# Rewritten stage boundaries of a three-block network kernel on one core

## The chip, the cores and the metric

The kernel runs on one core of a Trainium2 chip. The metric is device time in microseconds: how long one execution of the whole program takes on that core. Five engines work in it, each with an instruction stream of its own: TensorE (PE in the profile, with its weight loads as PEld), VectorE (DVE), ScalarE (ACT), GpSimd (POOL) and SyncE (SP), which here issues the DMAs.

## The reference, cut to what matters

Three networks are chained on one sequence of 512 positions and 1024 channels. Each begins or ends its stages with a norm over the channels, and nearly all the arithmetic is dense products of 1024-channel activations with weights.

```python
def rmsnorm(x, g):                       # the second block's differs in the eps alone
    return x * lax.rsqrt(jnp.mean(x * x, axis=-1, keepdims=True) + EPS) * g

def _layernorm(x, g, b):                 # third block
    mu, var = x.mean(-1), ((x - mu) ** 2).mean(-1)
    return (x - mu) * rsqrt(var + 1e-5) * g + b

def reference(x, ...):
    x = first_block(x, ...)    # rmsnorm, z = h @ w_in, convolution and sparse attention, FFN, gate
    x = second_block(x, ...)   # hyena mixer + FFN, rwkv mixer + FFN, final rmsnorm
    return third_block(x, ...)

def third_block(x, ...):
    u = x @ w_in + b_in                                   # split into the inputs of both mixers
    h_a = _head_layernorm(_mlstm_chunkwise(...)) * sigmoid(mo)
    h_b = _head_rmsnorm(_hgrn2_chunkwise(silu(hq), 1 - f, hi, log f)) * sigmoid(hg)   # 8 heads
    mixed = sigmoid(ga) * (h_a @ w_proj_a) + sigmoid(gb) * (h_b @ w_proj_b)
    x = _layernorm(ALPHA * x + mixed @ w_out, ln1_g, ln1_b)
    ffn = (silu(x @ w_ffn_gate) * (x @ w_ffn_up)) @ w_ffn_down
    return _layernorm(ALPHA * x + ffn, ln2_g, ln2_b)
```

## The kernel before

**Layout.** The activation `x` lies transposed in eight tiles of 128 channels by 512 positions. A product in float32 is made of three faster ones: every operand is split into a high half (`wh`, `h`, a rounded copy made by ACT) and a low half (`wl`, `l`, the rest, a subtraction on DVE), and `mm3` adds the products (`wh`,`h`), (`wh`,`l`) and (`wl`,`h`). The trace writes a product as its two inputs, so these read `h,wh`, `l,wh` and `h,wl`. A weight comes in chunks: `wsplit` (lines 151 to 157) loads 128 by 2048 numbers, 1 MB, into a raw tile `wraw`, of which there are three, and makes `wh` and `wl` of it, of which there are two each. `dense_steps` then runs over the eight input tiles `k` and the two column groups of a chunk, three matmuls each: 48 matmuls in a chunk. All loads stand in one queue on SP.

**What sets the order.** The Tile framework's scheduler places the instructions of each engine by its own estimate of time. Where the code says `manual_schedule` for an engine, that engine runs in the order of the code. Tiles lie in pools: a tile of a new pool that falls on the place of an old one waits until the old one's last reader is done. `phase` (lines 109 to 114) opens the weight pool, then the activation pool, then PSUM; it is opened once for the first block and the first half of the second, once in `block2b` for the last FFN of the second block, and once for the third block.

**The start.** `begin` (264 to 273) loads x0 and x1, then the first weight chunk `w1a`, then x2 to x7. `norm_split` splits every x into `h` and `l` (lines 190, 191), squares it on ACT (`sq`, line 218) and sums the squares on POOL (`sqa`, line 223); a matmul with a matrix of ones (`sqa,ones`) sums over the channels, and `rstd_of` makes the reciprocal root of it with one Newton step (194 to 203). The products don't wait for `rstd`, which is multiplied in later.

**Norms at the end of a stage.** `sumsq_soon` (236 to 244) is the same sum with the last tile's square sent to PE by itself, so that only it is late. ACT holds one table of functions, and another function's table costs an `ACT_TABLE_LOAD`; the reciprocal root needs one.

**HGRN2 heads.** `hgrn` runs eight heads in pairs. `head` is a generator that yields between its steps: scores of the diagonal, seven levels of a tree in which DVE masks a level into `hpt` and multiplies `hq` and `hk` by the decay, then the product with the values `po`, a copy `ho`, and the norm of the head: square on ACT, ones matmul, `rstd_of`, two products on DVE. `weave` (line 2127) mixes the steps of two heads with the matmuls of a fill (the input products of the next pair, 24 or 40 steps) by the counts it is given; PE alone runs there in the order of the code.

**Layer norms of the third block.** `LayerNorm` centres the tiles on the mean of the first six (`mean`, `center`), sums their squares on POOL (`lna`), and treats x6 and x7, which are late, apart (`late`): `p1` gathers the sum of the two, `p2` the squares. `finish` (1770 to 1782) takes the rest of the mean off all eight tiles (`dm`; the trace calls that tile `z`), five of them on DVE and three on POOL, makes the variance `w` (in the trace `ct`), then `rstd`, and then multiplies every tile by gain and `rstd` on DVE and adds the bias on ACT. After the first of them (LN1) the FFN splits the eight tiles (`split`, lines 187 and 188); after the second (LN2) they are stored.

## Time and profile before

| what | value |
|---|---|
| median of 3 runs | 4061.11 us (4058.75 to 4064.93) |
| the profiled execution | 4056.95 us, its span 4055.2 us |
| TensorE clock over the span | 0.967 of full |
| busy: PE / DVE / ACT / POOL | 94 / 59 / 40 / 18% |
| chain that ended last | PE 58%, DVE 8%, ACT 3% |

The span is the time from the first to the last instruction of the profiled execution. A row of the timeline gives the start of an instruction, its duration, engine and line, what it writes and reads, and in brackets how long the engine was idle before it and what ended that; rows marked x5 are five alike in a run, with the time from the first's start to the last's end. A window row gives busy time and number of instructions for each engine in a stretch, then the granted clock (1.00 is 2.4 GHz, 0.50 is 1.2 GHz) and the DMA share.

### The profile page before, as it was taken

The page shows a single profiled execution, that of the slowest core. Times are in us where ns is not written, and L with a number is a line of the kernel's source. Part 1 is how long each engine was busy: PE and PEld are TensorE (multiplying, and loading weights), DVE is VectorE, ACT ScalarE, POOL GpSimd, SP SyncE. Part 2 cuts the span into 40 slices and gives each one's busy share as a digit, 9 for nine tenths or more (in the row PEclk, how much of TensorE's full clock was granted, in tenths as well). Part 3 has the DMA queues.
Part 4 walks back from the last instruction along what each step waited for, and adds up shares of the span by engine and source line. Part 5 has one row for each costly group of instructions (what it writes and reads, how often), then busy time and mean ns, then how long its engine had stood idle before and what let it go on. Part 6 is the DMA issues. An engine that isn't in the chain of part 4 may idle for free.

```text
span 4055.2 us, 51969 instructions
## 1 busy us (share of the span) xinstructions
PE 3813.6 (94%) x20982; PEld 2972.9 (73%) x20982; DVE 2390.9 (59%) x3492; ACT 1610.3 (40%) x2182; POOL 726.5 (18%) x574
## 2 busy tenths in 40 slices
PE   8899999999899998889878899999999999998998
PEld 6556888777788883666656688877777888876886
DVE  5965655667866556476665665565554554454334
ACT  3455433455443333343442333355544333323222
POOL 1000200032620016444442100101111000030001
PEclk9899999999999999999988899999999999999999
DMA  6122222222232324544433223132223222332221
GB/s 214 48 78 98 100 86 106 90 94 94 99 110 88 106 82 156 150 112 112 117 92 103 99 78 115 57 136 93 86 93 117 86 79 78 130 127 73 99 87 64
DMA packets 184132, 408.69 MB, mean 101 GB/s; under 512 B 80361, under 2 KB 98314, under 8 KB 155988
## 3 DMA queue, kind: packets, MB, share of 16 engines
q1 hardware_dynamic: 183892, 405.38, 30.0%
q8 instruction: 165, 2.70, 0.3%
q14 instruction: 75, 0.61, 0.0%
HBM read 364.37 MB, written 43.57 MB: 101 GB/s over the span
## 4 chain that ended last, share of the span: by engine, by line
PE 58%; DVE 8%; ACT 3%; DMA 1%; issue 1%; POOL 0%; SPq 0%; DVEq 0%; ACTq 0%; POOLq 0%
PE pacc L138 49%; PE pf L138 3%; PE pb L138 2%; PE ch L138 1%; PE pa L138 1%; DVE ct L1928 1%; DVE wl L157 1%; DVE GB L1418 1%; DVE tw L1470 1%; PE py L138 1%; DVE W L1472 0%; ACT wh L156 0%; PE pb L1440 0%; DVE bk L1378 0%; DVE x L1776 0%
## 5 line engine op out<-in xcount | busy, mean ns | idle before, releaser
L138 PE MATMUL pacc<-h,wh 128*128 128x512 f32 x3792 | 1499.2, 397 | 34.1 <-ACT wh L156 19.9
L138 PE MATMUL pacc<-h,wl 128*128 128x512 f32 x3792 | 1484.7, 393 | 4.1 <-DVE wl L157 4.1
L138 PE MATMUL pacc<-l,wh 128*128 128x512 f32 x3792 | 1486.3, 392 | 1.3 <-DVE l L188 1.2
L138 PEld LDWEIGHTS pacc<-h,wh 128*128 128x128 f32 x3792 | 718.0, 189 | 215.1 <-issue 31.1
L138 PEld LDWEIGHTS pacc<-h,wl 128*128 128x128 f32 x3792 | 716.5, 189 | 163.4 <-DVE wl L157 8.4
L138 PEld LDWEIGHTS pacc<-l,wh 128*128 128x128 f32 x3792 | 717.9, 189 | 151.5 <-issue 3.4
L157 DVE TENSOR_TENSOR wl<-wraw,wh 128x2048 fp32r<-128x2048 f32 (+2 forms) x276 | 610.4, 2212 | 370.1 <-ACT wh L156 370.0
L156 ACT ACTIVATE wh<-wraw 128x2048 fp32r<-128x2048 f32 (+2 forms) x276 | 492.6, 1785 | 789.6 <-PE pacc L138 692.1
L138 PE MATMUL pf<-x,wf 128*128 128x256 f32 x736 | 222.2, 424 | 5.7 <-DMA x<-yd 3.4
L223 POOL TENSOR_TENSOR sqa<-sq 128x512 f32<-128x512 f32 x12 | 19.3, 1609 | 1007.7 <-ACT sq L218 667.8
L138 PEld LDWEIGHTS pf<-x,wf 128*128 128x128 f32 x736 | 131.2, 198 | 41.5 <-issue 11.4
L295 DVE TENSOR_TENSOR z<-pacc,rstd 128x512 f32<-128x512 f32 x132 | 90.2, 691 | 101.3 <-PE pacc L138 101.0
L323 DVE TENSOR_TENSOR x<-pacc,x 128x512 f32<-128x512 f32 x48 | 33.2, 691 | 178.4 <-PE pacc L138 178.4
L223 POOL TENSOR_TENSOR sqa<-sqa,sq 128x512 f32<-128x512 f32 x50 | 100.4, 2008 | 110.1 <-ACT sq L218 102.1
L309 ACT ACTIVATE ct<-ct 128x512 f32<-128x512 f32 x66 | 41.8, 633 | 180.8 <-DVE ct L306 120.4
L138 PE MATMUL pacc<-wh,h 128*128 128x512 f32 (+2 forms) x288 | 103.6, 362 | 9.6 <-DVE z L983 9.6
L1835 POOL TENSOR_TENSOR x<-x,z 128x512 f32<-128x512 f32 x16 | 22.8, 1447 | 456.4 <-DVE z L1834 456.4
L138 PE MATMUL pacc<-wl,h 128*128 128x512 f32 (+2 forms) x288 | 103.2, 358 | 0.4 <-DVE wl L157 0.4
L138 PE MATMUL pacc<-wh,l 128*128 128x512 f32 (+2 forms) x288 | 103.1, 361 | 0.0
L290 DVE TENSOR_TENSOR hv<-ct,pacc 128x512 f32<-128x512 f32 x22 | 15.1, 688 | 143.3 <-PE pacc L138 143.3
L552 DVE SCALAR_TENSOR_TENSOR x<-sg,vecs,x 128x491 f32<-128x491 f32 (+28 forms) x120 | 86.2, 744 | 5.1 <-ACT x L543 4.7
L1421 POOL TENSOR_TENSOR AX<-AX,rwc 64x512 f32<-64x512 f32 x64 | 82.3, 1286 | 33.3 <-ACT AX L1420 29.7
(521 smaller groups left out, 4997.2 us busy)
## 6 DMA issues: line engine op xcount, KB each, us to landing
wraw<-in_w_up_dram SPq DMA_DIRECT2D x44, 1024.0 KB, 4.8
wraw<-in_w_down_dram SPq DMA_DIRECT2D x32, 704.0 KB, 4.0
wraw<-in_w_up2a_dram SPq DMA_DIRECT2D x22, 1024.0 KB, 4.8
wraw<-in_w_up2b_dram SPq DMA_DIRECT2D x22, 1024.0 KB, 4.9
x<-xmd SPq DMA_DIRECT2D x72, 256.0 KB, 2.8
wraw<-in_w1a_dram SPq DMA_DIRECT2D x16, 1024.0 KB, 4.8
wraw<-in_w3q_dram SPq DMA_DIRECT2D x16, 1024.0 KB, 4.8
wraw<-in_hy_w_in_dram SPq DMA_DIRECT2D x12, 1024.0 KB, 4.7
```

Of the source, the lines that this page charges most:

```text
L138: s.nc.tensor.matmul(out, a, b, start=start, stop=stop)
L156: s.nc.scalar.activation(wh[:, :n], raw[:, :n], AF.Copy)
L157: s.nc.vector.tensor_tensor(wl[:, :n], raw[:, :n], wh[:, :n].bitcast(F), op=SUB)
L223: nc.gpsimd.tensor_tensor(a2, acc, q, op=ADD)
L295: nc.vector.tensor_tensor(z, ps, rstd, op=MUL)
L309: nc.scalar.activation(t, t, act)
L323: nc.vector.tensor_tensor(x[n], ps, x[n], op=ADD)
L552: nc.vector.scalar_tensor_tensor(y[:, d:], u[:, :T - d], w, y[:, d:], op0=MUL, op1=ADD)
L1418: nc.vector.tensor_tensor(GB[h, hs], q[h], mask[h, None].to_broadcast([64, 4, 2, 64]), op=MUL)
L1421: nc.gpsimd.tensor_tensor(AX[o, hs, X], AX[o, hs, X], mask[o, None].to_broadcast([64, 4, 2, 64]), op=MUL)
L1470: nc.vector.tensor_tensor(tw[:, 0:i, 0:i], W[:, 0:i, 0:i].rearrange("p j c -> p c j"), L[:, 0:i, i][:, None, :].to_broadcast([P, i, i]), o ...
L1928: nc.vector.scalar_tensor_tensor(t[:, d:], z[:, :T - d], w[3 - d], t[:, d:], op0=MUL, op1=ADD)
```

## The change

It has five parts, and all keep the arithmetic of the outputs up to the order of additions.

1. `begin` loads the first weight in four pieces of 256 KB, one after each even x tile, and splits each piece by itself. A small activation on `ones` stands first on ACT and brings the table load before the data.
2. `phase` can open the activation pool before the weight pool (`weights_last`), and does in two of the three phases. In `block3` the first weight of mLSTM, `w3q`, is loaded and split ahead of the splits of x.
3. `ready`, an activation on one column with the reciprocal root, brings that function's table in early: in `sumsq_soon`, LN1 and LN2.
4. In `head` of `hgrn` the square is issued with the copy of `po`, and the ones matmul three yields later; `weave` is told 24 steps instead of 22.
5. `LayerNorm.finish` is written out: four tiles are shifted on POOL and four on DVE, of which two before the variance and two between its steps; for LN1 it makes `h` straight from the product plus bias on ACT and `l` on DVE tile by tile, and the biased x last. LN1 with the last chunk before it, and the end of LN2, run in the order of the code on PE, DVE and ACT. In `p2` the early part comes ahead of x7's.

```diff
     def phase(s, wbufs=(3, 2), weights_last=False):
...
+            if weights_last:
+                s.ap, s.wp = pool("apool"), pool("wpool")
+            else:
+                s.wp, s.ap = pool("wpool"), pool("apool")
...
+    def ready(s, x):
+
+        t = s.ap.tile([P, 1], F, name="rdy", tag="rdy", bufs=1)
+        s.nc.scalar.activation(t, x[:, 0:1], AF.Abs_reciprocal_sqrt, scale=0.0, bias=s.eps(1.0))
+
     def sumsq_soon(s, xs):
 
         acc = s.sumsq_of(xs[:-1])
+        s.ready(xs[-2])
...
     def begin(s):
...
+        t = s.ap.tile([P, 1], F, name="rdy", tag="rdy", bufs=1)
+        nc.scalar.activation(t, s.ones[:, 0:1], AF.Copy)
...
+        for i in range(4):
+            a = slice(512 * i, 512 * i + 512)
+            nc.sync.dma_start(x[2 * i], s.I["xT"][2 * i])
+            nc.sync.dma_start(raw[:, a], s.I["w1a"][0][:, a])
+            nc.sync.dma_start(x[2 * i + 1], s.I["xT"][2 * i + 1])
+            nc.scalar.activation(wh[:, a], raw[:, a], AF.Copy)
+            nc.vector.tensor_tensor(wl[:, a], raw[:, a], wh[:, a].bitcast(F), op=SUB)
         s.constants()
...
-    with s.phase():
+    with s.phase(weights_last=True):
...
         s.k.mm(s.p1, s.k.ones, s.x[n], n == 6, n == 7)
-        s.k.mm(s.p2, s.k.ones, s.last.pop(n), n == 6, False)
+        s.k.mm(s.p2, s.k.ones, s.last.pop(n), n == 6, n == 7)
 
     def early(s):
-        s.k.mm(s.p2, s.k.ones, s.q, False, True)
+        s.k.mm(s.p2, s.k.ones, s.q, False, False)
...
+    def finish(s, g, b, split=False):
...
+        def shift(n):
+            (nc.vector if n < 4 else nc.gpsimd).tensor_tensor(s.x[n], s.x[n], dm, op=SUB)
+
         nc.scalar.activation(dm, s.p1, AF.Copy, scale=1.0 / 1024)
         nc.scalar.activation(w, s.p1, AF.Square, scale=1.0 / 1024)
+        for n in (4, 5, 6, 7, 0, 1):
+            shift(n)
+        nc.vector.scalar_tensor_tensor(w, s.p2, 1.0 / 1024, w, op0=MUL, op1=SUB)
+        nc.scalar.activation(r, w, AF.Abs_reciprocal_sqrt, bias=k.eps(1e-5))
+        nc.vector.tensor_scalar(v, w, 1.0, 1e-5, op0=MUL, op1=ADD)
+        shift(2)
+        nc.scalar.activation(u, r, AF.Square)
+        nc.vector.scalar_tensor_tensor(u, u, -0.5, v, op0=MUL, op1=MUL)
+        nc.vector.scalar_tensor_tensor(r, u, 1.5, r, op0=ADD, op1=MUL)
...
+            if n == 2:
+                shift(3)
             nc.vector.scalar_tensor_tensor(x, x, k.v(g, n), r, op0=MUL, op1=MUL)
-            nc.scalar.activation(x, x, AF.Identity, bias=k.v(b, n))
+            if split:
+                out.append([k.ap.tile([P, T], R, name=i, tag="xs", bufs=16) for i in "hl"])
+                nc.scalar.activation(out[n][0], x, AF.Identity, bias=k.v(b, n))
+                if n:
+                    low(n - 1)
...
+    w = s.wsplit("w3q", 0, 8, 256)
     xs = [s.split(x[n], "xs", 8) for n in range(NT)]
...
-        ln.late(6)
-        ln.late(7)
-        ln.early()
-        ln.finish("ln1_g", "ln1_b")
+            s.ready(x[7])
+            ln.late(6)
+            ln.early()
+            ln.late(7)
+            xs = ln.finish("ln1_g", "ln1_b", split=True)
...
+    with tc.manual_schedule(engines=MANUAL):
+        s.ready(x[7])
+        ln.early()
         ln.late(7)
-        ln.early()
-    ln.finish("ln2_g", "ln2_b")
+        ln.finish("ln2_g", "ln2_b")
...
         nc.scalar.activation(o, po, AF.Copy)
-        yield
-        r = s.rstd_of(s.sumsq([o]), 1.0 / 128, 1e-6)
+        sq = s.sumsq_of([o])
+        yield
+        yield
+        yield
+        r = s.rstd_of(s.spread(sq), 1.0 / 128, 1e-6)
...
-            weave((head(2 * j), 22), (head(2 * j + 1), 22), (fill, (24, 40, 24, TAIL)[j]))
+            weave((head(2 * j), 24), (head(2 * j + 1), 24), (fill, (24, 40, 24, TAIL)[j]))
```

How it moves the instructions is shown at three places. First ACT at the start of the program, before; `wh` on one 1 MB chunk stands between `h` of x1 and of x2:

```order
L190 ACT_TABLE_LOAD
L190 ACTIVATE h<-x,vecs 128x512
L218 ACTIVATE sq<-x 128x512 x2
L190 ACTIVATE h<-x,vecs 128x512
L156 ACTIVATE wh<-wraw 128x2048
L190 ACTIVATE h<-x,vecs 128x512
L218 ACTIVATE sq<-x 128x512
L190 ACTIVATE h<-x,vecs 128x512
```

and after:

```order
L279 ACT_TABLE_LOAD
L279 ACTIVATE rdy<-ones 128x1
L195 ACTIVATE h<-x,vecs 128x512
L223 ACTIVATE sq<-x 128x512
L289 ACTIVATE wh<-wraw 128x512
L195 ACTIVATE h<-x,vecs 128x512
L223 ACTIVATE sq<-x 128x512
L195 ACTIVATE h<-x,vecs 128x512
L289 ACTIVATE wh<-wraw 128x512
L223 ACTIVATE sq<-x 128x512
L195 ACTIVATE h<-x,vecs 128x512
```

The big `wh` has become four small ones spread among the `h` and `sq` of all eight tiles; DVE's `wl` is spread among its `l` in the same way, after l0, l2, l3 and l5.

Second, ACT at the end of the second pair of HGRN2 heads, before; `ho` is the copy of a head's product, `sq` its square, `rstd` and `rs` its reciprocal root:

```order
L2114 ACTIVATE ho<-pacc 128x512
L197 ACT_TABLE_LOAD
L197 ACTIVATE rstd<-pacc,eps_171 128x512
L200 ACTIVATE rs<-rstd 128x512
L218 ACTIVATE sq<-ho 128x512
L197 ACTIVATE rstd<-pacc,eps_171 128x512
```

and after:

```order
L2169 ACTIVATE ho<-pacc 128x512 x2
L223 ACTIVATE sq<-ho 128x512 x2
L202 ACT_TABLE_LOAD
L202 ACTIVATE rstd<-pacc,eps_182 128x512
L205 ACTIVATE rs<-rstd 128x512
L202 ACTIVATE rstd<-pacc,eps_182 128x512
```

The second head's square no longer stands behind the first head's `rstd`, for which ACT waits on PE.

Third, DVE through LN1, before; line 1743 centres x6 and x7, line 157 makes a `wl` of the FFN's second chunk, line 1776 is the shift by `dm`, 1777 the variance, 1781 gain and `rstd`, 188 the `l` of the FFN's input:

```order
L1743 TENSOR_TENSOR x<-x,z 128x512
L157 TENSOR_TENSOR wl<-wraw,wh 128x2048
L1743 TENSOR_TENSOR x<-x,z 128x512
L1776 TENSOR_TENSOR x<-x,z 128x512 x5
L1777 SCALAR_TENSOR_TENSOR ct<-pacc,ct 128x512
L198 TENSOR_SCALAR ct<-ct 128x512
L201 SCALAR_TENSOR_TENSOR ct<-ct 128x512
L202 SCALAR_TENSOR_TENSOR rstd<-ct,rstd 128x512
L1781 SCALAR_TENSOR_TENSOR x<-x,vecs,rstd 128x512 x8
L188 TENSOR_TENSOR l<-x,h 128x512 x8
```

and after (1763 centres, 1797 shifts, 1803 to 1809 variance and root, 1818 gain and `rstd`, 1813 `l`):

```order
L1763 TENSOR_TENSOR x<-x,z 128x512
L162 TENSOR_TENSOR wl<-wraw,wh 128x2048
L1797 TENSOR_TENSOR x<-x,z 128x512 x2
L1803 SCALAR_TENSOR_TENSOR ct<-pacc,ct 128x512
L132 MEMSET eps_27086 128x1
L1805 TENSOR_SCALAR ct<-ct 128x512
L1797 TENSOR_TENSOR x<-x,z 128x512
L1808 SCALAR_TENSOR_TENSOR ct<-ct 128x512
L1809 SCALAR_TENSOR_TENSOR rstd<-ct,rstd 128x512
L1818 SCALAR_TENSOR_TENSOR x<-x,vecs,rstd 128x512 x2
L1813 SCALAR_TENSOR_TENSOR l<-x,vecs,h 128x512
L1797 TENSOR_TENSOR x<-x,z 128x512
```

Three shifts have left the stretch ahead of the variance (one to POOL, two to later places), both centrings stand ahead of `wl`, and `l` follows its x at a distance of one tile instead of coming after all eight.

Elsewhere the scheduler has put DVE and ACT of the sparse attention, which the diff does not touch, into another order. At the beginning of the third block SP issues the first two `w3q` chunks ahead of the small loads of the gates (`c3`, `wif`).

## Rows read from the trace of the kernel before

**Rows 1.** Page, the chain that ended last: share of the span by engine.

```profile
PE 58%; DVE 8%; ACT 3%; DMA 1%; issue 1%; POOL 0%; SPq 0%; DVEq 0%; ACTq 0%; POOLq 0%
```

**Rows 2.** Timeline, 0 to 30 us: start, duration, engine, line, operation [idle before].

```profile
12.86 0.79 PE L138 MATMUL pacc<-h,wh 128*128 128x512 f32 x1 [12.86 <-ACT wh L156]
...
25.39 0.50 PE L138 MATMUL pacc<-l,wh 128*128 128x512 f32 x1
...
28.79 0.50 PE L138 MATMUL pacc<-h,wh 128*128 128x512 f32 x1
...
10.90 1.91 ACT L156 ACTIVATE wh<-wraw 128x2048 fp32r<-128x2048 f32 x1 [3.29 <-DMA wraw<-in_w1a_dram]
...
15.05 10.28 DVE L191 SCALAR_TENSOR_TENSOR l<-x,vecs,h 128x512 fp32r<-128x512 f32 x6
...
14.09 10.70 POOL L223 TENSOR_TENSOR sqa<-sqa,sq 128x512 f32<-128x512 f32 x6 [5.75 <-ACT sq L218]
```

**Rows 3.** Windows: stretch, then busy us (count) of each engine, PEclk, DMA share, GB/s.

```profile
10.00:16.00 6.00, 2.88 (x6) 1.87 (x7) 3.16 (x2) 4.79 (x6) 1.91 (x1) 1.00 1.03 368
...
120.00:140.00 20.00, 15.35 (x64) 10.30 (x63) 20.00 (x52) 8.19 (x15) 1.29 (x1) 0.73 0.15 54
```

**Rows 4.** Waits of PE, 28 to 240 and 3190 to 3400 us: total, times, longest.

```profile
PE pacc L673 <- DVE pt L647: 11.1, 3, 7.5
...
PE pacc L138 <- ACT sq L218: 5.9, 3, 2.0
```

**Rows 5.** Timeline, ACT and DVE at the second pair of HGRN2 heads, 3282 to 3306 us.

```profile
3286.97 0.69 ACT L197 ACTIVATE rstd<-pacc,eps 128x512 f32<-128x512 f32 x1 [1.42 <-PE pacc L138]
...
3288.23 0.61 ACT L218 ACTIVATE sq<-ho 128x512 f32<-128x512 f32 x1
...
3299.56 2.29 DVE L157 TENSOR_TENSOR wl<-wraw,wh 128x2048 fp32r<-128x2048 f32 x1
...
3305.71 0.73 DVE L2079 COPY_PREDICATED hpt<-c3m,pacc 128x256 f32<-128x256 uint16 x1 [1.41 <-PE pacc L138]
```

**Rows 6.** Windows behind an HGRN2 wait and behind LN1 (columns as in rows 3).

```profile
3290.00:3300.00 10.00, 10.00 (x47) 8.42 (x46) 8.21 (x15) 7.50 (x8) 0.00 (x0) 0.84 0.24 81
...
3661.90:3675.50 13.60, 8.06 (x18) 5.89 (x19) 11.67 (x18) 10.59 (x18) 0.00 (x0) 0.50 0.00 1
```

**Rows 7.** Timeline, LN1, 3638 to 3690 us: POOL, PE, ACT, DVE.

```profile
3641.99 8.34 POOL L1738 TENSOR_TENSOR lna<-lna,lnq 128x512 f32<-128x512 f32 x4
...
3650.93 2.07 PE L138 MATMUL pacc<-x,ones 128*128 128x512 f32 x2 [2.86 <-DVE x L1743]
...
3666.22 2.08 PE L138 MATMUL pacc<-h,wh 128*128 128x512 f32 x4 [9.57 <-ACT h L187]
...
3653.04 0.60 ACT L1773 ACTIVATE z<-pacc 128x512 f32<-128x512 f32 x1 [1.44 <-PE pacc L138]
...
3653.67 6.30 DVE L1776 TENSOR_TENSOR x<-x,z 128x512 f32<-128x512 f32 x5 [2.79 <-ACT z L1773]
...
3663.47 5.39 DVE L1781 SCALAR_TENSOR_TENSOR x<-x,vecs,rstd 128x512 f32<-128x512 f32 x8
...
3668.78 1.89 DVE L188 TENSOR_TENSOR l<-x,h 128x512 fp32r<-128x512 f32 x3
```

**Rows 8.** Timeline, LN2 at the end, 4030 to 4056 us: ACT, DVE.

```profile
4035.41 0.60 ACT L1773 ACTIVATE z<-pacc 128x512 f32<-128x512 f32 x1 [0.40 <-PE pacc L138]
...
4042.26 0.68 DVE L1777 SCALAR_TENSOR_TENSOR ct<-pacc,ct 128x512 f32<-128x512 f32 x1
...
4045.84 5.39 DVE L1781 SCALAR_TENSOR_TENSOR x<-x,vecs,rstd 128x512 f32<-128x512 f32 x8
```

**Rows 9.** Timeline, end of the second block, 2639 to 2658 us: ACT, PE.

```profile
2641.81 1.28 ACT L197 ACT_TABLE_LOAD   x1
2643.10 0.69 ACT L197 ACTIVATE rstd<-pacc,eps 128x512 f32<-128x512 f32 x1
...
2647.00 9.26 PE L138 MATMUL pacc<-x,wif 128*36 128x512 f32 x16 [4.04 <-DVE x L1720]
```

More of the change, by code (lines that the diff above doesn't have):

```diff
@@ L108, in phase @@
     @contextmanager
-    def phase(s, wbufs=(3, 2)):
+    def phase(s, wbufs=(3, 2), weights_last=False):
         s.wbufs = wbufs
-        with s.tc.tile_pool(name="wpool", bufs=1) as s.wp, s.tc.tile_pool(name="apool", bufs=1) as s.ap, \
-                s.tc.tile_pool(name="psum", bufs=1, space=bass.MemoryType.PSUM) as s.ps:
+        with ExitStack() as ctx:
+            pool = lambda n: ctx.enter_context(s.tc.tile_pool(name=n, bufs=1))
+            if weights_last:
+                s.ap, s.wp = pool("apool"), pool("wpool")
+            else:
+                s.wp, s.ap = pool("wpool"), pool("apool")
+            s.ps = ctx.enter_context(s.tc.tile_pool(name="psum", bufs=1, space=bass.MemoryType.PSUM))
             yield
@@ L264, in begin, with ffn @@
     def begin(s):
-        x, w = [], None
-        for n in range(NT):
-            if n == 2:
-                w = s.wsplit("w1a", 0, 8, 256)
-            x.append(s.xtile())
-            s.nc.sync.dma_start(x[n], s.I["xT"][n])
+        nc = s.nc
+        t = s.ap.tile([P, 1], F, name="rdy", tag="rdy", bufs=1)
+        nc.scalar.activation(t, s.ones[:, 0:1], AF.Copy)
+        x = [s.xtile() for n in range(NT)]
+        raw = s.wp.tile([P, 2048], F, name="wraw", tag="wraw", bufs=s.wbufs[0])
+        wh = s.wp.tile([P, 2048], R, name="wh", tag="wh", bufs=s.wbufs[1])
+        wl = s.wp.tile([P, 2048], R, name="wl", tag="wl", bufs=s.wbufs[1])
+        for i in range(4):
[5 more added lines that the diff above has]
+            nc.vector.tensor_tensor(wl[:, a], raw[:, a], wh[:, a].bitcast(F), op=SUB)
         s.constants()
-        return x, w
-    def ffn(s, x, xs, rstd, wup, wdown, act, conv=None, update=None, during=None):
+        return x, (wh.rearrange("p (k c) -> p k c", k=8), wl.rearrange("p (k c) -> p k c", k=8))
+    def ffn(s, x, xs, rstd, wup, wdown, act, conv=None, update=None, during=None, w=None):
         nc = s.nc
@@ L1725 @@
 TAIL = 64
+MANUAL = {mybir.EngineType.PE, mybir.EngineType.DVE, mybir.EngineType.Activation}
 class LayerNorm:
@@ L1773, in finish @@
         nc.scalar.activation(dm, s.p1, AF.Copy, scale=1.0 / 1024)
         nc.scalar.activation(w, s.p1, AF.Square, scale=1.0 / 1024)
-        for n, x in enumerate(s.x):
-            (nc.vector if n < 5 else nc.gpsimd).tensor_tensor(x, x, dm, op=SUB)
-        nc.vector.scalar_tensor_tensor(w, s.p2, 1.0 / 1024, w, op0=MUL, op1=SUB)
-        r = k.ap.tile([P, T], F, name="rstd", tag="rstd", bufs=2)
-        k.rsqrt(w, 1.0, 1e-5, k.tmp("ct"), r, k.tmp("ct"))
-        for n, x in enumerate(s.x):
-            nc.vector.scalar_tensor_tensor(x, x, k.v(g, n), r, op0=MUL, op1=MUL)
-            nc.scalar.activation(x, x, AF.Identity, bias=k.v(b, n))
+        for n in (4, 5, 6, 7, 0, 1):
+            shift(n)
@@ new lines, in finish, with low @@
+        nc.vector.scalar_tensor_tensor(w, s.p2, 1.0 / 1024, w, op0=MUL, op1=SUB)
[5 more added lines that the diff above has]
+        nc.vector.scalar_tensor_tensor(r, u, 1.5, r, op0=ADD, op1=MUL)
+        out = []
+        def low(n):
+            nc.vector.scalar_tensor_tensor(out[n][1], s.x[n], k.v(b, n), out[n][0].bitcast(F), op0=ADD, op1=SUB)
@@ L1785, in block3 @@
+        if split:
+            low(7)
+            for n, x in enumerate(s.x):
+                nc.scalar.activation(x, x, AF.Identity, bias=k.v(b, n))
+        return out
 def block3(s, x):
@@ L1797, in block3 @@
         for h in range(4):
-            mlstm(s, bp, h, xs, ccol, rows, cst, hA)
+            mlstm(s, bp, h, xs, ccol, rows, cst, hA, None if h else w)
     with tc.tile_pool(name="b3h", bufs=1) as bp:
@@ L1911, in gates, with mlstm @@
     return ccol, (mt, rows[32:36])
-def mlstm(s, bp, h, xs, ccol, rows, cst, hA):
+def mlstm(s, bp, h, xs, ccol, rows, cst, hA, w0):
     nc, I = s.nc, s.I
@@ L1932, in mlstm @@
     for c in range(4):
-        s.dense("w3q", 4 * h + c, 8, 256, xs, evac_qk, 2 * c)
+        s.dense("w3q", 4 * h + c, 8, 256, xs, evac_qk, 2 * c, w=None if c else w0)
     pn = s.ms()
@@ L2380, in body @@
         x = block2b(s, x)
-        with s.phase():
+        with s.phase(weights_last=True):
             x = block3(s, x)
```

33 lines of the change are left out of this document (19 added, 14 removed).

## The prediction

> **What bounds the kernel now.** Read the chain of waits first: PE carries 58% of it, DVE 8% and ACT 3% [rows 1]. TensorE is busy for 94% of the span, and the change takes away none of its matmuls. So it can only win back stretches in which PE stands still or runs at half clock, and each must be looked at in its own place. The timeline shows three of them that the change touches.
>
> At the start PE stands for 12.86 us until `wh` is made; ACT had waited 3.29 us for the 1 MB chunk before it, and made `wh` from 10.90 on. Behind it DVE makes l2 to l7 in 10.28 us while POOL adds squares for 10.70 us, 1.71 us each and in step, and PE takes `l` of x7 at 25.39, 12.5 us after its first matmul. The second chunk starts at 28.79 [rows 2].
>
> In the HGRN2 stage PE waits three times for the square of a head, 5.9 us in all [rows 4]. The timeline of the second pair shows why: ACT executes in order, the first head's `rstd` waits there for PE (1.42 us), and the second head's square, 3288.23, stands behind it, while PE waits for that square [rows 5]. After such a wait the granted clock is down: 0.84 over the next 10 us [rows 6].
>
> At LN1 PE waits 2.86 us for the centred x7 and 9.57 us for the first `h` of the FFN; behind that it runs at half clock, 0.50 over 13.6 us, and waits for the first `l`, because all eight `l` stand behind eight products and the first is made at 3668.78 [rows 6, 7].
>
> **The change part by part.** All sums are against the profiled execution, 4056.95 us. It lies 4.2 us under the median of the runs shown; at the end I take the saving off the median, 4061.11.
>
> *The start.* ACT's work there is eight `h` and `sq` and, in place of one `wh`, four quarters of it. With the first quarter there after the first x tile PE starts earlier, but it can't end the chunk earlier than `l` of x7 comes. DVE has eight `l` of at most 1.71 us (13.7) and a quarter of `wl` four times; I price a quarter like `wh`, 1.91/4, with the half as much again that a DVE operation beside POOL pays, 0.7, so 2.8 in all. From `h` of x0 at about 5.3 us (its table load moves ahead of the data, so not later) that is 16.5 us, less 1.5 for the first two, which have no POOL beside them: 20.3 us, against 25.39 before [rows 2]. What PE does between `l` of x7 and the second chunk stays (one sum over squares, four small products); the last triplet of matmuls now stands ahead of the sum, which changes nothing. So the second chunk starts about 5.1 us earlier, and a little more, 5.5, since POOL and DVE overlap less than fully. Bounds: 4 if the DMAs are what is late (the queues are full from 10 to 16 us, share 1.03, 368 GB/s [rows 3]: 3 MB at that rate take 8.5 us, so x7 lands between 12 and 14), 7 if half of the `l` run without POOL.
>
> *Pool order and early weights.* At both places the first load of the new phase still waits for the last matmul of the old one, since no order of pools frees the raw tile sooner. I price it at nothing. At the third block's start PE works on the gates from 2647.00, when x is normalized [rows 9]; the small `wif` now stands behind 1 MB of weights and may land just after that: between -0.3 and +1.0, taken 0.
>
> *Early tables in `sumsq_soon`.* The load ran from 2641.81 to 2643.09, beside the ones matmul that `rstd` waits for, and `rstd` started at 2643.10 [rows 9]. Nothing is gained: 0 to 0.1. The Trainium skill ("ScalarE: Activation LUTs", section "What ACT_TABLE_LOAD costs") says that a switch takes 1.283 us for the load and 1.38 us for a drain, 2.66 in all. The first figure is this trace's; of the second the next activation shows nothing, 0.01 us behind the load. By the page, each load that now stands ahead of `dm` in a layer norm would cost 1.4 us more than in my sum, about 1.4 us in LN2 alone, where ACT is late.
>
> *HGRN2.* With the squares of both heads ahead of the `rstd`, and the ones matmuls a few triplets of fill behind `po`, the 5.9 us go: a square needs 0.6 us and the fill covers that. The cover is there, since the fill's matmuls are only moved, from later in the pair to earlier. What comes back of the clock: 16% of 10 us at two of the three places, 1.6 each [rows 6], so up to 3.2. Against it, fill that is spent here is missing at the levels. There DVE has little room: with a `wl` of 2.29 us ahead of a level it still waited 1.41 us for PE in that period [rows 5]. Sum 5.9 + 1.6 = 7.5, half of the clock; bounds 4 and 9.
>
> *LN1.* Until `dm` nothing is won: x7 is centred earlier, but its sum now stands behind the one that waits for POOL's chain, which ends at 3650.33, and at half clock each takes 2.07 us [rows 7]. So `dm` starts between 3653 and 3654.5, against 3653.04. From `dm` to the first matmul it was 13.2 us. Now two shifts beside POOL (1.70 each), not five in 6.30, stand before the variance: `dm` 0.6, shifts 3.4, variance 0.7, the third shift 1.7 while ACT makes the root, three small steps 1.8, product 0.7, `h` 0.7: 9.7 to 10.3, PE at 3663 to 3664.5 instead of 3666.22. Then the larger part: `l` of x0 follows at once, where it came at 3668.78 after 5.39 us of products [rows 7], and the pair of DVE operations per tile, 0.67 and 0.63, is faster than six matmuls of PE at half clock. PE runs through from 3665 instead of 3669.5: 4.5 us. With a shorter pause the half clock may end a little earlier: 5. Bounds 3 and 7. The biases on ACT that follow have no reader before the FFN's end.
>
> *LN2.* The table load, hidden before, now stands ahead of `dm`, and the order of the sums puts one more in front of `p1`; the load's 1.28 us [rows 9], with a little of it covered, makes `dm` 4036.5 instead of 4035.41. Two shifts instead of five bring the variance from 4042.26 to 4040.5. From there to the first product it was 3.58 us; the third and fourth shifts, on DVE still beside POOL, give back 1.2 to 2 of the 1.8 that were won [rows 8]. I take 0.5, bounds -0.5 and 1.9.
>
> *Attention.* The scheduler's new order of DVE moves single operations by some 3 us either way. DVE is full there, 20.00 of 20 us at 120 us [rows 3], and PE waits for it, 11.1 us at one line [rows 4]. The sum of DVE's work is the same, and so is its end: 0, bounds -4 and +4.
>
> Sum: 5.5 + 7.5 + 5 + 0.5 = 18.5 us. Profiled execution 4038.5, median **4042.5 us**.
>
> **The rivals.** *The start's gain is swallowed.* The attention stage is DVE's. If it is bound by DVE from the first `l` on and not from when PE brings the scores, or if its new order takes the upper bound, the 5.5 us are gone when it ends: 13 us saved, 4048. For it: the 20.00 of 20. Against it: at the start PE, not DVE, hands on the work, and DVE's load there is made earlier too.
>
> *The waits change places.* In HGRN2 the levels run out of fill and take 4 us back, LN1's end is held by the chain of small steps, so that only 2 come of it, and the start brings its lower bound: 3.5 + 2 + 4 = 9.5, of which attention takes 2.5: about 7, 4054, within what can't be told from no change. For it: what was won is in front of serial chains in each place.
>
> *Slower.* The weave is one order by hand for 28 level steps (four pairs, seven levels). With 24 steps instead of 22 and fill spent behind `po`, a level's matmuls can come before DVE has finished the masks and products of the level before. DVE's room is the 1.41 us of the row [rows 5]; where a 2.29 us `wl` falls in front of a level without fill to cover it, PE waits about 0.9 us, and the clock falls with it as after the other waits, 1.6 us each time. If that meets 12 of 28 steps, 12 x 2.5 = 30 us against a gain of 11 elsewhere: 4080. It decides from about 8 steps on. Against it: DVE is empty for most of such a period and the number of `wl` is unchanged.
>
> *The table switch drains.* By the page's price LN2 loses 1 us and the time is 4044; the rows speak against it.
>
> **How the numbers follow.** The forecast gets 0.57, the swallowed start 0.17, the waits that change places 0.14, slower 0.06, the drain 0.02; 0.04 is for a larger gain, all upper bounds at once (7 + 9 + 7 + 2 + 4 = 29), 4032. About 0.2% (8 us) is what a measurement of this kernel can tell from no change. Faster by more: 0.57 + 0.17 + 0.02 + 0.04 = 0.80, less 0.02 for the spread of the runs, some 6 us: 0.78. Within: 0.16. Slower: 0.06. The range goes from the upper bounds, 4032, to the case of the changed places with 2 us of spread, 4056; the likeliest case alone has 4037 to 4047.
>
> **What would show it.** Right: the second chunk starts near 23.5 us; PE has no wait for `sq` of a head and the windows after it show a clock near 1; LN1's pause of PE ends 9.7 to 10.3 us after `dm`, and no wait for `l` follows; the last product of LN2 ends within a microsecond of its place relative to the last matmul. Wrong: waits of PE for `hpt` or `hq` that weren't there, more than 25 us of waits for DVE between 120 and 240 us, or a wait for `wraw` behind the first chunk.

## The result, and the profile after

The changed kernel took **4096.43 us** (median of 4 runs, 4089.01 to 4099.2), the kernel before 4059.93 us on the same chip. The ratio is 1.009, with an interval of 1.0077 to 1.0102: slower by some 37 us, where 18.5 us less were forecast, and far outside the range.

PE's waits are not what grew; its busy time did, from 3813.6 to 3879.6 us. These are the products in the groups of the page after, in the columns line, engine, operation, shape, count, then busy time, mean ns of one, and idle time before it:

```profile
L143 PE MATMUL pacc<-h,wh 128*128 128x512 f32 x3792 | 1517.8, 402 | 26.5 <-ACT h L1821 9.2
L143 PE MATMUL pacc<-l,wh 128*128 128x512 f32 x3792 | 1504.6, 397 | 3.0 <-DVE l L196 2.8
L143 PE MATMUL pacc<-h,wl 128*128 128x512 f32 x3792 | 1502.0, 397 | 3.4 <-DVE wl L162 3.4
```

The same three groups before:

```profile
L138 PE MATMUL pacc<-h,wh 128*128 128x512 f32 x3792 | 1499.2, 397 | 34.1 <-ACT wh L156 19.9
L138 PE MATMUL pacc<-h,wl 128*128 128x512 f32 x3792 | 1484.7, 393 | 4.1 <-DVE wl L157 4.1
L138 PE MATMUL pacc<-l,wh 128*128 128x512 f32 x3792 | 1486.3, 392 | 1.3 <-DVE l L188 1.2
```

As many matmuls, some 5 ns longer each. In dense stretches that no edit touches this is plain to see. Windows of 80 us in the first block's FFN, PE without a pause; the count in brackets is the number of matmuls. Before, then after:

```profile
620.00:700.00 80.00, 80.00 (x355) 66.24 (x354) 46.87 (x52) 29.80 (x30) 0.00 (x0) 1.00 0.30 106
```

```profile
620.00:700.00 80.00, 80.00 (x344) 64.27 (x343) 46.29 (x51) 27.43 (x28) 0.00 (x0) 1.00 0.30 106
```

Full clock (1.00), no wait, equal DMA traffic (106 GB/s), and 344 matmuls in place of 355. From start to start a product took 227 ns before and 233 after. (Step times here and below are means over neighbouring matmuls in the trace, steps over 260 ns left out.) That the order of the work is not the cause, the runs below show.

What differs there is **where the operands lie**. `rdy`, one float in each partition, is allocated in the activation pool ahead of `h` and `l`, and takes 32 bytes. In the compiled program before, all 12000 products of 512 columns between two split operands (11952 of them between `h` or `l` and `wh` or `wl`) have both operands at the same place modulo 256 bytes. After, 5904 are 32 bytes apart, 4992 are 224 apart (modulo 256, where the activation pool comes first), and 1104 are in step, nearly all of them the down products of the last two FFNs, whose inputs lie in another pool. (`phase` is opened a fourth time, for the second block's mixer, which the description of the kernel leaves out; `rdy` stands there too.) Read by that distance, the steps of the trace after take 233.3 ns at 32, 233.3 at 224, and 226.8 at 0. 10896 matmuls by some 6.2 ns are 68 us.

The stages that the prediction spoke of, in the trace after. The start (timeline; PE, DVE, POOL), to be compared with [rows 2]:

```profile
6.09 0.80 PE L143 MATMUL pacc<-h,wh 128*128 128x512 f32 x1 [6.09 <-ACT wh L289]
...
20.47 0.51 PE L143 MATMUL pacc<-l,wh 128*128 128x512 f32 x1 [1.70 <-DVE l L196]
...
25.02 0.50 PE L143 MATMUL pacc<-h,wh 128*128 128x512 f32 x1
...
16.96 1.77 DVE L290 TENSOR_TENSOR wl<-wraw,wh 128x512 fp32r<-128x512 f32 x1
18.65 2.42 DVE L196 SCALAR_TENSOR_TENSOR l<-x,vecs,h 128x512 fp32r<-128x512 f32 x2
...
10.09 9.78 POOL L228 TENSOR_TENSOR sqa<-sqa,sq 128x512 f32<-128x512 f32 x6 [1.08 <-ACT sq L223]
```

PE starts 6.8 us earlier, and the second chunk 3.8 us. DVE is what is late: a quarter of `wl` beside POOL takes 1.77 us, as long as an `l` there, and PE's last wait in the chunk, 1.70 us up to 20.47, is for the `l` of x6 that stands behind it.

Waits of PE in the attention stage and in HGRN2, after ([rows 4]):

```profile
PE pacc L692 <- DVE pt L666: 11.3, 3, 7.0
...
PE pacc L143 <- ACT hk L2104: 1.4, 2, 0.7
PE pacc L143 <- DVE hq L2121: 0.4, 1, 0.4
```

The waits for the square of a head are gone, and 1.8 us of others came. LN1 after ([rows 7]): the last product ahead of it, the sums of x6 and of x7, the first product of the FFN, `dm`, the split of the second chunk on DVE, POOL's squares:

```profile
3686.17 0.40 PE L143 MATMUL pacc<-h,wl 128*128 128x512 f32 x1
...
3687.95 1.12 PE L143 MATMUL pacc<-x,ones 128*128 128x512 f32 x2 [1.38 <-DVE x L1763]
...
3693.24 1.02 PE L143 MATMUL pacc<-x,ones 128*128 128x512 f32 x2
...
3704.35 2.07 PE L143 MATMUL pacc<-h,wh 128*128 128x512 f32 x4 [9.23 <-ACT h L1821]
...
3694.29 0.60 ACT L1799 ACTIVATE z<-pacc 128x512 f32<-128x512 f32 x1 [1.32 <-PE pacc L143]
...
3689.51 3.35 DVE L162 TENSOR_TENSOR wl<-wraw,wh 128x2048 fp32r<-128x2048 f32 x1
...
3684.04 6.66 POOL L1758 TENSOR_TENSOR lna<-lna,lnq 128x512 f32<-128x512 f32 x4
```

To be compared with the kernel before, beside [rows 7]: the last product and the sum of x6:

```profile
3640.83 0.39 PE L138 MATMUL pacc<-h,wl 128*128 128x512 f32 x1
3645.99 2.08 PE L138 MATMUL pacc<-x,ones 128*128 128x512 f32 x2 [4.78 <-DVE x L1743]
```

From `dm` to the first product it is 10.06 us, as forecast; and no wait for `l` follows. LN2 after ([rows 8]):

```profile
4077.03 0.63 ACT L1765 ACTIVATE lnq<-x 128x512 f32<-128x512 f32 x1 [1.04 <-POOL lna L1758]
4077.67 1.28 ACT L244 ACT_TABLE_LOAD   x1
4078.97 0.29 ACT L244 ACTIVATE rdy<-x,eps 128x1 f32<-128x1 f32 x1
4079.17 0.58 ACT L1799 ACTIVATE z<-pacc 128x512 f32<-128x512 f32 x1
...
4079.78 2.36 DVE L1797 TENSOR_TENSOR x<-x,z 128x512 f32<-128x512 f32 x2 [3.91 <-ACT z L1799]
4082.06 0.68 DVE L1803 SCALAR_TENSOR_TENSOR ct<-pacc,ct 128x512 f32<-128x512 f32 x1
...
4087.64 1.42 DVE L1818 SCALAR_TENSOR_TENSOR x<-x,vecs,rstd 128x512 f32<-128x512 f32 x2
```

The variance comes 2.9 us after `dm` instead of 6.85, and the first product 5.6 us after the variance instead of 3.6: what was won in front is mostly given back behind.

### The profile page after: what moved, and what is told of

The parts are those of the page before. It is cut to its first block, busy times and chain, and to the rows that moved or that the text cites. A ratio compares the mean times of both kernels' runs of the same rounds, so it can differ in the third digit from the quotient of the medians.

```text
span 4097.4 us, 51975 instructions
## 1 busy us (share of the span) xinstructions
PE 3879.6 (95%) x20982; PEld 2978.0 (73%) x20982; DVE 2389.7 (58%) x3493; ACT 1613.5 (39%) x2190; POOL 730.8 (18%) x576
## 4 chain that ended last, share of the span: by engine, by line
PE 79%; DVE 10%; ACT 3%; issue 2%; DMA 2%; POOL 1%; SPq 0%; DVEq 0%; ACTq 0%; POOLq 0%
PE pacc L143 70%; PE pf L143 3%; PE pb L143 2%; PE ch L143 1%; DVE wl L162 1%; PE pa L143 1%; DVE x L571 1%; DVE GB L1437 1%; DVE tw L1489 1%; PE py L143 1%; ACT wh L161 1%; PE pacc L692 0%; DVE W L1491 0%; PE pb L1459 0%; DMA x<-rid 0%
## 5 line engine op out<-in xcount | busy, mean ns | idle before, releaser
L143 PE MATMUL pacc<-h,wh 128*128 128x512 f32 x3792 | 1517.8, 402 | 26.5 <-ACT h L1821 9.2
L143 PE MATMUL pacc<-l,wh 128*128 128x512 f32 x3792 | 1504.6, 397 | 3.0 <-DVE l L196 2.8
L143 PE MATMUL pacc<-h,wl 128*128 128x512 f32 x3792 | 1502.0, 397 | 3.4 <-DVE wl L162 3.4
L162 DVE TENSOR_TENSOR wl<-wraw,wh 128x2048 fp32r<-128x2048 f32 (+1 forms) x275 | 609.7, 2217 | 370.0 <-ACT wh L161 369.9
L161 ACT ACTIVATE wh<-wraw 128x2048 fp32r<-128x2048 f32 (+1 forms) x275 | 490.5, 1784 | 815.2 <-PE pacc L143 735.5
L571 DVE SCALAR_TENSOR_TENSOR x<-sg,vecs,x 128x499 f32<-128x499 f32 (+28 forms) x120 | 85.6, 739 | 4.8 <-ACT x L562 4.4
```

The lines of the kernel that those rows point to most:

```text
L143: s.nc.tensor.matmul(out, a, b, start=start, stop=stop)
L161: s.nc.scalar.activation(wh[:, :n], raw[:, :n], AF.Copy)
L162: s.nc.vector.tensor_tensor(wl[:, :n], raw[:, :n], wh[:, :n].bitcast(F), op=SUB)
L571: nc.vector.scalar_tensor_tensor(y[:, d:], u[:, :T - d], w, y[:, d:], op0=MUL, op1=ADD)
```

## The experiments

Two theories stood against each other at first. A: the place of the operands against each other sets the pace of the matmuls. B: another order, or weights loaded earlier, slows PE. Except where said, the kernels keep the order of instructions of the kernel that they start from.

**The changed kernel with a longer rdy tile.**

```diff
-        t = s.ap.tile([P, 1], F, name="rdy", tag="rdy", bufs=1)
+        t = s.ap.tile([P, 128], F, name="rdy", tag="rdy", bufs=1)[:, 0:1]
```

> The changed kernel with its one-column tile rdy widened from 4 to 512 bytes in each partition, of which one column is used; the order of instructions on all five engines is that of the changed kernel. Theory A (place of the operands): in the changed kernel h and l lie 32 bytes off from wh and wl modulo 64, and its matmuls start every 234 ns instead of 227; here the offset is a multiple of 512 again, so 227 ns return on some 10,700 matmuls, 67 us: about 4030 us. Theory B (order or traffic: another order on the engines or earlier weight loads slow PE down): nothing moves here, so 4096 us and 234 ns.

Measured: 4037.82 us (4028.31 to 4045.2), ratio to before 0.995 (0.9935 to 0.9966). The same window:

```profile
620.00:700.00 80.00, 80.00 (x354) 66.26 (x354) 51.03 (x57) 30.28 (x32) 0.00 (x0) 1.00 0.30 103
```

Before took 4058.59 us on that chip. 508 bytes more in one tile turn 36.5 us of loss into 20.8 us of gain, each against the kernel before on its own chip: some 57 us, with all instructions in the same order. Theory B falls. Between the two profiled executions it is 67.5 us. Where PE waits for others anyway, a longer product costs less: up to the first FFN, attention included, some 900 of them would make 5.6 us, and 1.2 show. The second block's mixer takes between 814 and 830 us in the profiled executions of all the runs, whatever the kernel, so the 10 us between 57 and 67.5 can't be placed from one execution of each.

**The kernel before with 32 bytes of padding.** In `phase`, for the three phases that hold FFNs, attention and the third block:

```diff
+            if pad:
+                s.nc.gpsimd.memset(s.ap.tile([P, pad], F, name="pad", tag="pad", bufs=1), 0.0)
```

> The kernel before with a pad of 32 bytes ahead of the activations' pool in the three phases that hold the FFNs, attention and the third block; same order of instructions but for one memset in each. Theory A: all products of activations and weights run at 234 ns, some 11,900 of them, 75 us: about 4135 us. Theory B: 4061 us.

Measured: 4119.09 us (4117.09 to 4123.01), ratio 1.0153 (1.0139 to 1.0166), and 344 matmuls in the window:

```profile
620.00:700.00 80.00, 80.00 (x344) 64.30 (x343) 44.16 (x48) 26.92 (x26) 0.00 (x0) 1.00 0.29 105
```

An unused tile of 32 bytes alone makes the kernel before 60 us slower. That is theory A. Of the 75 us expected 15 don't show in the medians; up to the first FFN the profiled execution loses 0.6 us where 5.6 were due, so waits of PE hide a part, and the rest is not traced.

**Weights and activations shifted together.** The pad of 32 bytes stands first in the weight pool of every phase:

```diff
+            s.nc.gpsimd.memset(s.wp.tile([P, 8], F, name="pad", tag="pad", bufs=1), 0.0)
             yield
```

> The kernel before with a pad of 32 bytes ahead of the weights in every phase, which shifts the weights and the activations alike. Theory A (offset between the two): 227 ns, 4061 us. Theory C (the place of the activations itself, a multiple of 64 or not): 234 ns on all products, about 4135 us.

Measured: 4057.99 us against 4058.59, ratio 0.9997 (0.9986 to 1.0008), 227 ns, and in the window

```profile
620.00:700.00 80.00, 80.00 (x355) 66.24 (x354) 47.15 (x52) 30.07 (x30) 0.00 (x0) 1.00 0.29 106
```

It is the distance between the two, not the place itself.

**Which distances are slow?** Pads of 64, 128 and 256 bytes (16, 32 and 64 floats) in the three phases, and later 128, 192 and 64. For the first of the two, in the order of the file:

```diff
-    with s.phase():
+    with s.phase(pad=32):
...
-        with s.phase():
+        with s.phase(pad=16):
...
-        with s.phase():
+        with s.phase(pad=64):
```

> The kernel before with a pad of 64 bytes ahead of the activations in the first phase, 128 in the phase of the second block's last FFN, 256 in the third block. Read: the time from matmul to matmul in each phase. If only the offset modulo 64 counts, 227 ns in all three and about 4061 us. If it counts modulo 128, 234 ns in the first phase alone (about 4900 matmuls, 34 us: 4095 us); modulo 256, in the first two; modulo 512, in all three.

Measured: 4064.81 us (one run). Windows in the three phases:

```profile
620.00:700.00 80.00, 80.00 (x351) 65.64 (x350) 46.94 (x52) 27.73 (x28) 0.00 (x0) 1.00 0.30 106
...
2460.00:2540.00 80.00, 80.00 (x346) 64.83 (x346) 49.80 (x57) 29.46 (x31) 0.00 (x0) 1.00 0.30 106
3850.00:3930.00 80.00, 80.00 (x355) 66.24 (x354) 27.46 (x22) 21.44 (x20) 0.00 (x0) 1.00 0.28 100
```

64 bytes cost a little (229.2 ns on 5018 steps), 128 the most of it (232.4 on 1559), 256 nothing (227.1 on 4316). A rule that only the distance modulo 64 counts, as I had it in the first expectation, falls, and so does one of 128; what is left is 256, with 64 bytes in between.

> The kernel before with other pads ahead of the activations: 128 bytes in the first phase, 192 in that of the second block's last FFN, 64 in the third block. With 64, 128 and 256 in this order the steps had taken 229.2, 232.4 and 227.1 ns. If the offset modulo 256 sets the pace, whatever the phase, then 128 gives 232 to 233 ns in the first phase, 64 gives 229 ns in the third block, and 192 some 231 to 235 ns: about 5000 x 5.5 + 1600 x 5.5 + 4300 x 2 = 45 us, 4103 us. If the phase and not the offset was what differed, the first phase has 229 ns again and the third block 227: about 4077 us.

Measured: 4115.48 us (one run), with

```profile
620.00:700.00 80.00, 80.00 (x345) 64.34 (x344) 42.45 (x46) 26.92 (x26) 0.00 (x0) 1.00 0.30 106
2460.00:2540.00 80.00, 80.00 (x345) 64.11 (x344) 40.45 (x42) 23.80 (x23) 0.00 (x0) 1.00 0.31 107
3850.00:3930.00 80.00, 80.00 (x345) 64.79 (x344) 25.18 (x21) 17.99 (x14) 0.00 (x0) 1.00 0.30 106
```

232.7 ns for 128, 233.3 for 192, 231.0 for 64. For 128 bytes, read in two phases, the distance decides and not the phase. For 64 bytes the two runs differ, 229.2 in the first phase and 231.0 in the third block, and why is open; it is also why the run lost 53 us and not the 45 expected.

Then the weights 16 bytes off:

```diff
-        wh = s.wp.tile([P, 2048], R, name="wh", tag="wh", bufs=s.wbufs[1])
-        wl = s.wp.tile([P, 2048], R, name="wl", tag="wl", bufs=s.wbufs[1])
+        wh = s.wp.tile([P, 2064], R, name="wh", tag="wh", bufs=s.wbufs[1])[:, 4:2052]
+        wl = s.wp.tile([P, 2064], R, name="wl", tag="wl", bufs=s.wbufs[1])[:, 4:2052]
```

> The kernel before with wh and wl both 16 bytes further in their tiles; order of instructions unchanged. So far the pace was 227 ns with the operands 0, 64, 128 or 256 bytes apart modulo their tiles, and 234 ns with 32. If any offset that is no multiple of 64 is slow, 234 ns or more on all products and about 4120 us. If only the 32-byte half of a 64-byte line counts, 227 ns and 4059 us.

Measured: 4114.64 us (one run). The expectation counts 64 and 128 bytes as fast, against the 229.2 and 232.4 ns that had just been read; that part was wrong when it was written. The slots of `wh` and `wl` had also become 64 bytes longer, so that nearly all distances modulo 256 were 48, 112, 176 and 240, mixed within each triple; they took 231.4 to 234.6 ns. Taken together: 0 modulo 256 is fast, 227 ns; 64 lies between; 32, 128, 192 and 224, read by themselves, take 232 to 233, and 48, 112, 176 and 240, read only among each other, 231 to 235.

**Whose distance?** Three kernels put one operand alone out of step. The first two were not clean. First `wl`:

```diff
-        wl = s.wp.tile([P, 2048], R, name="wl", tag="wl", bufs=s.wbufs[1])
+        wl = s.wp.tile([P, 2064], R, name="wl", tag="wl", bufs=s.wbufs[1])[:, 8:2056]
```

> The kernel before, with wl alone put 32 bytes further in its tile, so that one of three products (h,wl) has its operands 32 bytes apart and the other two have not. If what counts is the matmul's own pair, the step from h,wl to the next matmul takes 234 ns and the other two 227: 3792 x 7 = 26 us, 4085 us. If it is the next weights, loaded while another product's activations are read, the step that is long is the one from l,wh to h,wl, and the total is the same. If weights do not count, 227 everywhere and 4059 us.

Measured: 4108.4 us (one run), and all three steps long, 231.4 to 233.4 ns. Neither reading of mine fits; the compiled program tells why: the longer slots of `wl` moved `h` and `l` by 128 bytes against `wh` as well.

Then `l`, in `split`:

```diff
-        h = pool.tile([P, T], R, name="h", tag=tagh, bufs=2 * bufs)
-        l = pool.tile([P, T], R, name="l", tag=tagh, bufs=2 * bufs)
+        h = pool.tile([P, T + 8], R, name="h", tag=tagh, bufs=2 * bufs)[:, 0:512]
+        l = pool.tile([P, T + 8], R, name="l", tag=tagh, bufs=2 * bufs)[:, 0:512]
```

> The kernel before with the tiles of h and l 32 bytes longer, so that in each pair l lies 32 bytes off from h; in 2056 of 3792 triples l,wh alone has its operands 32 bytes apart, in the other 1736 h,wh and h,wl have. With wl alone shifted, all three steps had become slow, most of all the two ends of h,wl. If any change of place among the operands of neighbouring matmuls is enough, all steps take 231 to 234 ns here too, 4110 to 4120 us. If it is the matmul's own pair after all, one step of three in the first kind and two in the second take 234 ns: 5500 x 7 = 38 us, 4098 us.

Measured: 4100.7 us (one run), steps of 231 to 232 ns throughout. Here too more was moved than meant: with slots of 2080 bytes the distances run through all multiples of 32. What it adds: a matmul in step among others that mostly are not took 232.1 ns.

The third keeps the slots at a multiple of 256 bytes:

```diff
-        wl = s.wp.tile([P, 2048], R, name="wl", tag="wl", bufs=s.wbufs[1])
+        wl = s.wp.tile([P, 2112], R, name="wl", tag="wl", bufs=s.wbufs[1])[:, 8:2056]
```

> The kernel before with wl alone 32 bytes further, in tiles whose length is a multiple of 256 bytes, so that h and l stay 0 modulo 256 against wh and only h,wl has its operands 32 bytes apart. (The earlier shift of wl had made the slots 8256 bytes long, so that h and l moved by 128 bytes against wh as well, and all three products were off.) If it is the matmul's own pair, the step from h,wl to h,wh takes 233 ns and the two others 227: 3792 x 6 = 23 us, 4081 us. If it is the weights that are loaded meanwhile, the step from l,wh to h,wl is long, with the same total. If one product that is off slows the whole row, 231 to 234 ns in all and about 4115 us.

Measured: 4116.44 us (one run). The groups of 500 to 700 us, busy time, mean ns of one:

```profile
L138 PE MATMUL pacc<-l,wh 128*128 128x512 f32 x285 | 114.0, 400 | 0.0
L138 PE MATMUL pacc<-h,wh 128*128 128x512 f32 x286 | 112.8, 395 | 0.0
L138 PE MATMUL pacc<-h,wl 128*128 128x512 f32 x285 | 110.8, 389 | 0.3 <-DVE wl L157 0.3
```

From l,wh to h,wl it takes 238.3 ns, from h,wh to l,wh 232.3, from h,wl to h,wh 228.7; on average 233.1, as if all were out of step. One product in three that is off costs as much as three. The longest step is the one that ends with the product that is off, but its neighbours are slower than 227 too. So it is not the own pair alone. Of the three readings expected, the total is that of the third (one product slows the whole row), while the step that is longest is the one that the second named (the weights that are loaded meanwhile); none fits as a whole. What in the chip does it stays open.

**The parts of the change by themselves.** No rdy at all, order otherwise as in the changed kernel:

```diff
-        t = s.ap.tile([P, 1], F, name="rdy", tag="rdy", bufs=1)
-        nc.scalar.activation(t, s.ones[:, 0:1], AF.Copy)
...
-        t = s.ap.tile([P, 1], F, name="rdy", tag="rdy", bufs=1)
-        s.nc.scalar.activation(t, x[:, 0:1], AF.Abs_reciprocal_sqrt, scale=0.0, bias=s.eps(1.0))
+        pass
```

> The changed kernel without rdy: the early table loads of the start, of the sums of squares and of both layer norms are gone, and so is the 4-byte tile; the order is otherwise that of the changed kernel. If the early tables are worth nothing and only the tile's place cost time, the time is that of the run with the wide tile, 4038 us, within 2 us (LN2 gets about 1 us back, the start loses some). If the early tables bring something, up to 1.3 us at each of five places: 4044 us. If the loss is not the tile's: 4096 us.

Measured: 4039.61 us (4037.32 to 4043.59), ratio 0.9949 (0.9936 to 0.9961): as fast as with the long tile. Followed from matmul to matmul, the profiled execution is 1.1 us behind that of the long tile at the first product and 1.8 at the 1600th, and loses nothing more in the FFNs, in the third block, in LN1 or LN2 (in the second block's mixer, between the two, it loses 10 us more, within the spread of that stage). So in this pair the table load at the start is worth 1 to 2 us and the other `rdy` nothing; the medians of the two runs, 20.8 us under before in both, don't show a difference. This kernel keeps the new order of the pools, and all its 12000 products are in step: the order of the pools alone moves nothing. That load kept, in a tile that exists anyway:

```diff
+        t = s.ap.tile([P, T], F, name="rdy", tag="nrm", bufs=4)[:, 0:1]
+        nc.scalar.activation(t, s.ones[:, 0:1], AF.Copy)
```

> The changed kernel with the early table load of the start kept, but written into a tile that exists anyway (a slot of the squares), and without the other three rdy. No tile is added. Theory: the start's table load is worth 1 to 2 us, the others nothing, and the operands lie as before: 4036 to 4039 us, as fast as the run with the wide tile.

Measured: **4032.3 us** (4030.53 to 4044.93), before 4057.22 on the same chip, ratio 0.9946 (0.9931 to 0.996). This version beats both kernels; its interval doesn't tell it apart from the runs without `rdy` and with the long one, and its profiled span, 4030.0 us, is that of the long one (4029.9).

The HGRN2 part alone in the kernel before:

```diff
+        sq = s.sumsq_of([o])
+        yield
+        yield
         yield
-        r = s.rstd_of(s.sumsq([o]), 1.0 / 128, 1e-6)
+        r = s.rstd_of(s.spread(sq), 1.0 / 128, 1e-6)
...
-            weave((head(2 * j), 22), (head(2 * j + 1), 22), (fill, (24, 40, 24, TAIL)[j]))
+            weave((head(2 * j), 24), (head(2 * j + 1), 24), (fill, (24, 40, 24, TAIL)[j]))
```

> The kernel before with the part on the HGRN2 heads alone: squares issued with the copies, ones matmul three yields later, 24 steps. Theory: 5.9 us of waits for the square go, and a part of the clock behind them, 7 us: 4052 us. Rival: the levels run out of fill and take it back: 4057 to 4060 us, with new waits of PE in the stage.

Measured: 4053.42 us against 4060.38, ratio 0.9981 (0.9972 to 0.999): 7 us. From matmul to matmul the profiled one gains 6.8 us through the stage. PE's waits there:

```profile
PE pacc L138 <- ACT hk L2049: 1.5, 2, 0.7
PE pacc L138 <- DVE hq L2066: 0.6, 2, 0.4
PE pacc L138 <- DVE hk L2083: 0.2, 1, 0.2
```

The 5.9 us are gone and 1.9 us of new waits stand in their place (before it was 0.4), which leaves 4.0. The rest goes with the granted clock, which no longer falls; the stage before, then with this part alone:

```profile
3200.00:3400.00 200.00, 193.75 (x1037) 164.70 (x1036) 108.80 (x221) 75.41 (x83) 0.00 (x0) 0.98 0.23 81
```

```profile
3203.00:3403.00 200.00, 197.65 (x1065) 168.33 (x1064) 111.19 (x229) 74.84 (x83) 0.00 (x0) 1.00 0.26 88
```

LN1 in the order of the code, with the old `finish`:

```diff
-        for c in range(4):
-            for i, _ in enumerate(s.dense_steps("w_out3", c, 8, 256, ms, evac_x, 2 * c)):
-                if (c, i) == (3, 2):
-                    ln.mean()
+        for c in range(3):
+            s.dense("w_out3", c, 8, 256, ms, evac_x, 2 * c)
+        wo = s.wsplit("w_out3", 3, 8, 256)
+        with tc.manual_schedule(engines={mybir.EngineType.PE, mybir.EngineType.DVE, mybir.EngineType.Activation}):
+            for i, _ in enumerate(s.dense_steps("w_out3", 3, 8, 256, ms, evac_x, 6, w=wo)):
+                if i == 2:
+                    ln.mean()
...
```

> The kernel before with LN1 and the last chunk ahead of it in the order of the code on PE, DVE and ACT, and the old finish: on DVE the centring of x7 comes before the split of the FFN's second chunk. Theory: of the 12 us that the changed order saves around LN1, 5 lie ahead of dm and come from this order (x7 centred some 3 us sooner, POOL's chain free of the split, PE's clock not down): 4054 us and dm 6.5 us after the last matmul of the stage instead of 11.8. Rival: all of it is the new finish, or the other order of the sums: 4059 us.

Measured: 4055.17 us against 4060.38, ratio 0.9983 (0.9974 to 0.9993). The last product, x7's sum and `dm`, then the `wl` that now stands behind both centrings:

```profile
3648.52 0.39 PE L138 MATMUL pacc<-h,wl 128*128 128x512 f32 x1
...
3653.92 1.92 PE L138 MATMUL pacc<-x,ones 128*128 128x512 f32 x2
...
3655.87 0.60 ACT L1773 ACTIVATE z<-pacc 128x512 f32<-128x512 f32 x1 [2.02 <-PE pacc L138]
...
3651.99 3.35 DVE L157 TENSOR_TENSOR wl<-wraw,wh 128x2048 fp32r<-128x2048 f32 x1
```

`dm` starts 7.35 us after the start of the last product. In the kernel before the last product started at 3640.83 (shown above) and `dm` at 3653.04 [rows 7], 12.2 us. From matmul to matmul 5.75 us are won around LN1, all of it with the old finish.

## Why the prediction was wrong

**The step that failed** is the first one, that the change takes away none of PE's matmuls and so can only win back pauses: it took the duration of a matmul as given. The term that hid it is one that the prediction priced at nothing, the early tables. I counted `rdy` as a table load and one short activation on ACT, and looked for what else its instructions could delay. I did not count the place that the tile takes. Nearly all products of the FFNs, the projections and the third block read an operand from tiles that lie behind it or were moved by it, and 10896 of them became 6.2 ns longer: 68 us of PE time, some 57 us of the time of the program (36.5 us slower than before, and 20.8 us faster with the long tile). PE had little slack to hide it: it is busy for 94% of the span. The other term priced at nothing, the order of the pools, was right: without `rdy` it leaves all operands in step. None of its rivals had it; the one on the slow side, the levels of HGRN2, did not happen.

**The rest of the sum** can be judged with the places in step, by the kernel with the long rdy tile: 20.8 us faster by the medians, where 18.5 were forecast. That this is near is in good part luck: the start brought less than its lower bound and LN1 more than its upper one. In its profiled execution (span 4029.9 us, 25.3 us under that of before), followed from matmul to matmul:

| part | forecast | measured |
|---|---|---|
| start, up to the second chunk | 5.5 (4 to 7) | 3.55 |
| attention, up to the first FFN | 0 (-4 to 4) | 1.3 |
| pool order, tables, third block's start | 0 | about 0.6 |
| HGRN2 | 7.5 (4 to 9) | 6.8 |
| LN1 | 5 (3 to 7) | 12.35 |
| LN2 | 0.5 (-0.5 to 1.9) | 0.4 |

- *Start*: below its bound. In the trace after, DVE's work adds up as forecast, 14.96 us against 15.0, but by two errors that cancel: the quarters of `wl` took 4.92 instead of 2.8 (two of the four, beside POOL, 1.77 and 1.78), the `l` 10.04 instead of 12.2. With pauses in which DVE waits for ACT's `h`, `l` of x7 is done at 21.07, not at 20.3. It is not what PE waits for: the last wait is for `l` of x6, up to 20.47, and PE, busy with the products of x6, takes that of x7 at 21.97 only. So the second chunk starts at 25.02, not near 23.5.
- *HGRN2*: right in mechanism and size; the kernel with that part alone gives 7 us. Of its 6.8 us from matmul to matmul 4.0 are waits and 2.8 the clock, where the sum had 5.9 and 1.6.
- *LN1*: what came after `dm` was right, 10.06 us to the first product where 9.7 to 10.3 were forecast. The step "until `dm` nothing is won" was wrong: 12.2 us from the last product to `dm` became 8.1 in the trace after, and 7.35 with the order alone. I let POOL's chain end at 3650.33 as before, and let PE's sums run at half clock as before. But with the split of the second chunk behind both centrings, POOL adds four squares in 6.66 us instead of 8.34 [rows 7], PE pauses for 1.38 us and not for 4.78 and 2.86, and the granted clock over its sums is 0.80 (3686.4 to 3695 us) instead of 0.50 (3644.8 to 3655 before). The run of the order alone shows 5.75 us from this; the other 6.6 are the new finish, of which I had 5. In the run with the long tile, to which the table belongs, the clock over the sums is 1.00 and `dm` follows the last product by 6.85 us: 5.4 us are won ahead of `dm`, 3.1 from there to the first product, and 3.9 behind it.
- *LN2*: right, to a tenth of a microsecond; the third and fourth shifts give back most of what the first two won. The pieces were not: in the trace after the variance comes 3.96 us sooner behind `dm`, where 2.85 were taken, and the 2.0 that go again ahead of the first product are the most that was allowed.
- *Attention*: in the trace after 11.3 us of waits for DVE against 11.1, as taken; the run with the long tile wins 1.3 us there, inside the bounds.
- The Trainium skill ("ScalarE: Activation LUTs", "What ACT_TABLE_LOAD costs") adds 1.38 us of drain to the 1.283 us of a table load. In LN2 the square ahead of the load ends at 4077.66, the load runs from 4077.67 to 4078.95, `rdy` starts at 4078.97 and `dm` at 4079.17: no drain shows on either side, and the rival that rested on it falls.
